# Gated-unit operands loaded by halves: a reordering between retention and the gated unit of a one-core encoder kernel

## The chip, the cores and the metric

The kernel runs on one core of a Trainium2 chip, as one launch. The metric is the device time of a launch in microseconds (us); the median of several runs stands for a kernel. One further execution is taken with the hardware profiler, and all rows of profiles and traces are from that one.

The engines are named as the profile names them: PE is TensorE's matrix multiply (PEld its weight loads), DVE is VectorE, ACT is ScalarE, POOL is GpSimd, and SP is SyncE, whose queue issues all the DMAs of this kernel. L969 is line 969 of the kernel before.

## What is computed

The reference is a trunk of two layers on x of 1024 frames by 1024 channels, in float32. What matters here lies in the first layer. Its input projection gives several streams; one goes through a diagonal state-space layer (S5), a gelu and a gated unit (GLU), another through eight heads of chunkwise retention, and both are joined by an output projection:

```python
def s5_mixer(u, ...):            # ... states, then
    y = jax.nn.gelu(y)
    y = y * jax.nn.sigmoid(y @ glu_w + glu_b)      # the gated unit

def retention(q, k, v):          # per head, DK = 64, DV = 128
    q, k = rope(q) * DK ** -0.5, rope(k)
    scores = einsum('bnihd,bnjhd->bnhij', qc, kc) * intra
    kv = einsum('bnjhd,jh,bnjhe->bnhde', kc, k_dec, vc)
    # s_prev: running sum of kv, decayed from chunk to chunk
    out = scores @ vc + (qc * q_dec) @ s_prev       # then normalised per head

x = x + concatenate([y_s5 * silu(g_s5), y_ret * silu(g_ret)]) @ w_out
```

The second layer (a Conformer convolution module with gates) and a last RMSNorm follow.

## The kernel before

**Layout and products.** Channels lie on the 128 partitions, eight blocks of them (`kb` or `nb`), and frames along the free axis, in two halves of 512 (`h`). Matmuls run on a float32 format with fewer mantissa bits, so each operand is split into a high part (a rounded copy, made on ACT) and a low part (operand minus high part, made on DVE or POOL), and each product is three matmuls: high by high, high by low, low by high (`mm3`, L137 to L144, whose lines L142 to L144 are most of PE's time). `split` (L967 to L969) makes the two parts of an activation: the cast on ACT at L968, the subtraction on DVE at L969. `wload_pieces` (L122) does the same for a weight: a float32 tile `wf` of 128 by 1024 is loaded, cast to `wh` on ACT (L133) and its low part `wl` made on POOL or DVE (L134). `wnext` loads weights two ahead in a fixed list.

**What sets the order.** The kernel is written in a tile language whose scheduler places each engine's instructions in one fixed order, by priority (mostly the order of the program) and by its own estimate of when operands are there. `issue_after(ins)` keeps what is issued under it behind an instruction in that order. Each engine then runs its list strictly in order, and so does SP with its DMAs. A tile has a tag, and a tag has a number of buffers (`bufs`); a new tile waits until the last readers of the tile that had its buffer are done.

**The stretch of the change.** Retention works on pairs of heads (`retention`, L784). `ret_proj` (L809) makes one pair's keys, queries and values. Keys and queries are evacuated to `raw` (L822), four DMAs swap their quarters into `swp` (L831), POOL multiplies both by the rotation tables (L834, L835), and DVE adds them to `krot` and `qrot` (L836). The values are eight blocks of 24 matmuls each (L859 to L861), evacuated on ACT (L862); blocks 0 to 3 read half 0 of the layer's input `xs`, blocks 4 to 7 half 1. `swp` has one buffer. In the same function's wake `y_pass` (L775) loads the output of the S5 part for two channel blocks, takes the gelu on ACT into `yn` (L781, two buffers) and stores it to `yn_d`.

`ret_heads` (L865) then has PE transpose the keys (`ktp`, L874); DVE scales them by the decay (`kt`, L876); PE makes kv (L888), DVE accumulates it to S (L896, L898); PE makes the scores `sp` (L904), DVE masks them to `sc` (L910); PE makes the output from S and from `sc` (L930, L935); DVE normalises (L944 to L950); PE transposes back (L958), and DVE multiplies by the gate (L961).

After the fourth pair comes the gated unit in `layer0_back_and_layer1` (L971). `load_split(yn_d, "y", False)` (L981, L995 to L999) loads the eight rows of gelu output, each 128 by 1024, into buffers of the weights' tag `wf` (three buffers, shared with the weights), and splits each for half 0 and half 1. The operand tiles (`opA`, tags A0 and A1, 16 buffers each) are those that held `xs`: a half's tile comes free when the last V block that reads it has done so. The gated unit's matmuls (`mm_glu`) follow for eight weights and both halves. `yg` and `yn` (L1012 to L1016) are the gate and the gelu output, multiplied on POOL; `sg` (L1020, L1021) is the gate's result.

The scheduler lays the gated unit's first matmuls between the fourth pair's retention products, so that PE has work while DVE makes S and the scores. The loading and scaling of the convolution's weights `convw` (L1101, L1102) stand later in the program, but their load is free to go early, and the scheduler puts the scaling on DVE ahead of the low part `yl0_1`.

Last, `w_out` (L1032) makes x1, stores it, and `h1` (L1048) loads it back for the second layer: for half 0 into tiles of tag `u` (five buffers, eight rows, L1054), normalised by DVE (L1057). Weights used a second time have their low parts stored and loaded back (`wload_again`, L111, L119).

Of the kernel before, what the change touches and what calls it, by code (L numbers as in the profile page):

```python
# [3 lines left out]

# [7 lines left out]
F32 = mybir.dt.float32  # L12
# [27 lines left out]
class Trunk:  # L40
# [734 lines left out]
    def y_pass(self, rp, cb):  # L775

        nc = self.nc
        yt = rp.tile([P, 8, P], F32, name=f"yp_{cb}", tag="yp", bufs=1)
        nc.sync.dma_start(yt[:], self.y_d[cb].rearrange("i h g m -> (h g) i m"))
        yn = rp.tile([P, P, 8], F32, name=f"yn_{cb}", tag="ynt", bufs=2)  # L780
        nc.scalar.activation(yn[:], yt[:].rearrange("p i m -> p m i"), AF.Gelu_apprx_tanh)  # L781
        nc.sync.dma_start(self.yn_d[cb * P:(cb + 1) * P], yn[:].rearrange("p m i -> p (m i)"))

    def retention(self, st):  # L784
        nc, A = self.nc, self.A
        rp = self.rp = self.pool("ret", 1, stack=st)
        early = ExitStack()
        rq = self.rq = self.pool("retq", 1, stack=early, side="right")
        self.rk = rq.tile([P, 2, T], F32, name="ropek")
        nc.sync.dma_start(self.rk[:], A["rope_k"])  # L790
        self.mask = rp.tile([P, NH, P], F32, name="retmask")
        nc.sync.dma_start(self.mask[:], A["ret_mask"])
        self.kdec = rp.tile([P, NH, 64], F32, name="kdec")
        nc.sync.dma_start(self.kdec[:], A["ret_kdec"])
        self.g128 = rp.tile([P, 4], F32, name="g128")
        nc.sync.dma_start(self.g128[:], A["ret_g128"])
        for pair in range(4):
            cur = self.ret_proj(pair)
            with ExitStack() as held:
                if pair:  # L800
                    held.enter_context(self.tc.issue_after(self.last_rs.ins))
                for cb in (2 * pair, 2 * pair + 1):
                    self.y_pass(rq, cb)
            if pair == 3:
                early.close()
                self.lp = self.pool("l1", side="right")
            self.ret_heads(pair, *cur)

    def ret_proj(self, pair):  # L809
        nc, A, rp = self.nc, self.A, self.rp  # L810
        tq = self.rq.tile([P, 2, T], F32, name=f"ropeq_{pair}", tag="ropeq", bufs=1)
        nc.sync.dma_start(tq[:], A["rope_q"][pair])
        raws, tabs = {}, {"k": self.rk, "q": tq}

        def project(nm):
            w = self.wnext(f"{nm}{pair}")
            raw = raws[nm] = self.rq.tile([P, T], F32, name=f"{nm}raw_{pair}", tag="raw", bufs=2)
            for h in range(2):
                c = slice(h * HALF, (h + 1) * HALF)
                ps = self.bank(f"mm_{nm}{pair}_{h}", aux=False)  # L820
                self.gemm(ps[:], w, self.xs[h])
                last = nc.vector.tensor_tensor(raw[:, c], ps[:], self.R[:, c], op=ALU.mult)  # L822
            return last

        def turn(nm, behind=None):
            raw, tab = raws[nm], tabs[nm]
            swp = self.rq.tile([P, T], F32, name=f"{nm}swp_{pair}", tag="swp", bufs=1)
            o = rp.tile([P, T], F32, name=f"{nm}rot_{pair}", tag=f"{nm}rot", bufs=1)
            for b in range(4):
                s = b ^ 1  # L830
                nc.sync.dma_start(swp[32 * b:32 * b + 32, :], raw[32 * s:32 * s + 32, :])  # L831
            cs = [slice(h * HALF, (h + 1) * HALF) for h in range(2)]
            for c in cs:
                nc.gpsimd.tensor_tensor(raw[:, c], raw[:, c], tab[:, 0, c], op=ALU.mult)  # L834
                nc.gpsimd.tensor_tensor(swp[:, c], swp[:, c], tab[:, 1, c], op=ALU.mult)  # L835
            return o, [lambda c=c: nc.vector.tensor_tensor(o[:, c], raw[:, c], swp[:, c], op=ALU.add) for c in cs]  # L836


        project("k")
        krot, adds = turn("k")  # L840
        last = project("q")
        with self.tc.issue_after(last.ins):
            for add in adds:
                add()
        qrot, adds = turn("q")
        for add in adds:
            add()

        wv = [self.wnext(f"v{pair}_{i}") for i in range(2)]
        vt = rp.tile([P, 8, 256], F32, name=f"v_{pair}", tag="v", bufs=2)  # L850
        for b in range(8):
            ps = self.bank(f"mm_v{pair}_{b}", aux=False)
            h, o = b // 4, (b % 4) * P
            for kb in range(KB):
                xh, xl = self.xs[h][kb]
                i, k4 = kb // 4, kb % 4
                wh = wv[i][0][:].rearrange("p (k a) n -> p k (a n)", a=2)[:, k4, :]
                wl = wv[i][1][:].rearrange("p (k a) n -> p k (a n)", a=2)[:, k4, :]
                nc.tensor.matmul(ps[:, :256], xh[:, o:o + P], wh, start=kb == 0, stop=False)  # L859
                nc.tensor.matmul(ps[:, :256], xh[:, o:o + P], wl, start=False, stop=False)  # L860
                nc.tensor.matmul(ps[:, :256], xl[:, o:o + P], wh, start=False, stop=kb == KB - 1)  # L861
            nc.scalar.mul(vt[:, b, :], ps[:, :256], self.Rtok[:, b:b + 1])  # L862
        return krot, qrot, vt

    def ret_heads(self, pair, K, Q, V):  # L865
        nc, rp = self.nc, self.rp
        v = nc.vector

# [1 line left out]
        for hf in range(2):  # L870
            ps = self.bank(f"ktp{hf}_{pair}")
            for b in range(4):
                t0 = (4 * hf + b) * P
                nc.tensor.transpose(ps[:, b * P:(b + 1) * P], K[:, t0:t0 + P], self.ident[:])  # L874
            kd = self.kdec[:, 2 * pair:2 * pair + 2, :].rearrange("p h d -> p (h d)")
            v.tensor_tensor(kt[:, 4 * hf:4 * hf + 4, :], ps[:].rearrange("p (b d) -> p b d", b=4),  # L876
                            kd.unsqueeze(1).broadcast_to([P, 4, P]), op=ALU.mult)

        S = rp.tile([P, 8, P], F32, name=f"S_{pair}", tag="S", bufs=1)
        for hf in range(2):  # L880
# [83 lines left out]
            nc.sync.dma_start(self.yr_d[h * P:(h + 1) * P], gts[hh][:])  # L964


    def split(self, src, hi, lo, eng):  # L967
        self.nc.scalar.copy(hi[:], src)  # L968
        eng.tensor_tensor(lo[:], src, hi[:].bitcast(F32), op=ALU.subtract)  # L969

    def layer0_back_and_layer1(self, st):  # L971
        nc, A = self.nc, self.A
# [8 lines left out]
        def load_split(src, name, halves):  # L981
            res = [[], []]

            def put(kb, h, f):
                a, b = (self.op_tile(self.opA, f"A{h}", f"{name}{q}{kb}_{h}") for q in "hl")
                self.split(f, a, b, v)
                res[h].append((a, b))
            if halves:
                for h in range(2):
                    for kb in range(KB):  # L990
                        f = lp.tile([P, HALF], F32, name=f"{name}f{kb}_{h}", tag="tp", bufs=3)
                        nc.sync.dma_start(f[:], src[rows(kb), hs(h)])
                        put(kb, h, f[:])
            else:
                for kb in range(KB):  # L995
                    f = self.wp.tile([P, T], F32, name=f"{name}f{kb}", tag="wf", bufs=3)
                    nc.sync.dma_start(f[:], src[rows(kb)])
                    for h in range(2):
                        put(kb, h, f[:, hs(h)])  # L999
            return res  # L1000


# [6 lines left out]
        for nb, h in [(nb, h) for nb in range(6) for h in range(2)] + [(6, 0), (7, 0), (6, 1), (7, 1)]:  # L1009
# [11 lines left out]
            v.scalar_tensor_tensor(sg[:], sg[:], 1.0, yg[:], op0=ALU.add, op1=ALU.mult)  # L1021
            a, b = (self.op_tile(opB, f"B{h}", f"ys{q}{nb}_{h}") for q in "hl")
            nc.scalar.mul(a[:], sg[:], 0.5)
            v.scalar_tensor_tensor(b[:], sg[:], 0.5, a[:].bitcast(F32), op0=ALU.mult, op1=ALU.subtract)
            ys[h][nb] = (a, b)
        yr = load_split(self.yr_d, "yr", True)

# [20 lines left out]
        def h1(h):  # L1048
# [2 lines left out]
            res = []  # L1051
            for kb in range(KB):
                t = (opB.tile([P, HALF], F32, name=f"x1n{kb}_{h}", tag="B1") if h else
                     lp.tile([P, HALF], F32, name=f"x1n{kb}_{h}", tag="u", bufs=5))  # L1054
                nc.sync.dma_start(t[:], self.x1_d[rows(kb), hs(h)])
# [43 lines left out]

        cw = lp.tile([P, 8, CONV_K], F32, name="convw")  # L1100
        nc.sync.dma_start(cw[:], A["conv_w"])  # L1101
        v.tensor_scalar(cw[:], cw[:], 0.5, None, op0=ALU.mult)  # L1102
        cv = [[None] * 8 for _ in range(2)]
        zs = [[None] * 8 for _ in range(2)]
        NT = self.TAPS
# [334 lines left out]
```

## Time and profile before

| what | us |
|---|---|
| median of 3 runs | 1219.36 (1218.27 to 1221.7) |
| the profiled execution | 1219.24 |
| its span, first to last instruction | 1217.5 |
| mean granted TensorE clock | 0.997 |

The page gives, for each engine, its busy time and share of the span. The waits list who waited for whom: engine and line, what released it, us in total, how many times and the longest. A row of a timeline has start, length, engine, line, operation, output<-inputs, shapes and a count of merged instructions; in brackets is the engine's idle time before it and what ended that. A row of the chain has start, length, engine and what it was. In the groups by line, `x16 | 12.6, 821 | 3.3 <-ACT yh` means 16 instructions, 12.6 us busy, 821 ns on average, and 3.3 us of idle time before them, ended by ACT's `yh`. A row of a DMA group ends with the median us from issue to landing.

### The profile page before, as it was taken

How to read it: one execution, taken by the hardware profiler on the slowest of the kernel's cores; microseconds unless marked ns; L12 is line 12 of the kernel's file. 1: busy time of each engine (PE TensorE's matmuls, PEld its weight loads, DVE VectorE, ACT ScalarE, POOL GpSimd, SP SyncE). 2: the span in 40 equal slices, each digit the busy share in tenths (PEclk: the TensorE clock that was granted, in tenths of full speed). 3: DMA queues.
4: the chain of work that ended last, by engine and by line, in shares of the span. 5: the costliest groups of instructions: out<-in, count | busy, mean ns of one | idle time of the engine just before them, and what ended most of it. 6: DMA issues, size and time to landing. Idle time of an engine off the chain costs nothing.

```text
span 1217.5 us, 17581 instructions
## 1 busy us (share of the span) xinstructions
PE 1199.5 (99%) x6660; PEld 1011.3 (83%) x6660; DVE 747.1 (61%) x1337; ACT 480.6 (39%) x712; POOL 653.9 (54%) x453
## 2 busy tenths in 40 slices
PE   9999999999999999998999999999999999999997
PEld 7888888888889999997888888788888888888876
DVE  7965555555413635546746101599999799999533
ACT  7212233322222323134434322545545575434652
POOL 2059988888124333342454551578453467758642
PEclk9999999999999999999999999999999999999998
DMA  8342433333384536266446776755677654356764
GB/s 333 104 139 74 152 128 124 133 131 124 107 268 139 176 102 195 82 216 220 165 156 216 269 270 254 260 188 196 222 253 251 232 182 155 123 176 236 243 250 147
DMA packets 98500, 225.03 MB, mean 185 GB/s; under 512 B 9072, under 2 KB 38000, under 8 KB 97776
## 3 DMA queue, kind: packets, MB, share of 16 engines
q1 hardware_dynamic: 98416, 223.92, 54.9%
q8 instruction: 52, 0.85, 0.3%
q14 instruction: 32, 0.26, 0.1%
HBM read 158.41 MB, written 61.28 MB: 180 GB/s over the span
## 4 chain that ended last, share of the span: by engine, by line
PE 91%; DMA 4%; DVE 2%; ACT 1%; POOL 1%; issue 1%; SPq 1%; DVEq 0%; POOLq 0%
PE mm_g L143 7%; PE mm_g L144 7%; PE mm_g L142 7%; PE mm_wo L144 5%; PE mm_wo L142 5%; PE mm_wo L143 5%; PE mm_a L144 2%; PE mm_b L144 2%; PE mm_a L143 2%; PE mm_a L142 2%; PE mm_b L143 2%; PE mm_u L144 2%; PE mm_u L143 2%; PE mm_b L142 2%; PE mm_u L142 2%; PE mm_glu L144 2%
## 5 line engine op out<-in xcount | busy, mean ns | idle before, releaser
L1142 DVE SCALAR_TENSOR_TENSOR cv<-u,convw,cv 128x512 f32<-128x512 f32 x398 | 273.4, 751 | 11.9 <-ACT cv L1128 9.6
L1122 POOL TENSOR_TENSOR tp<-tp,tp 128x512 f32<-128x512 f32 x64 | 83.1, 1298 | 44.4 <-ACT tp L1121 43.3
L144 PE MATMUL mm_g<-xh,wl_g 128*128 128x512 f32 x256 | 100.8, 394 | 0.0
L143 PE MATMUL mm_g<-xl,wh_g 128*128 128x512 f32 x256 | 100.6, 393 | 0.0
L142 PE MATMUL mm_g<-xh,wh_g 128*128 128x512 f32 x256 | 100.5, 393 | 0.0
L861 PE MATMUL mm_v<-wh_v,xl 128*128 128x256 f32 x256 | 72.5, 283 | 0.0
L860 PE MATMUL mm_v<-wl_v,xh 128*128 128x256 f32 x256 | 72.4, 283 | 0.0
L859 PE MATMUL mm_v<-wh_v,xh 128*128 128x256 f32 x256 | 72.4, 283 | 0.0
L134 POOL TENSOR_TENSOR wl_v<-wf_v,wh_v 128x1024 fp32r<-128x1024 f32 x8 | 19.2, 2396 | 88.6 <-ACT wh_v L133 88.6
L1121 ACT ACTIVATE tp<-u,convw 128x512 f32<-128x512 f32 x64 | 45.7, 719 | 34.9 <-POOL tp L1122 33.2
L325 DVE TENSOR_TENSOR gt<-mm_g,R 128x512 f32<-128x512 f32 x32 | 21.9, 685 | 59.9 <-PE mm_g L144 59.9
L143 PEld LDWEIGHTS mm_g<-xl,wh_g 128*128 128x128 f32 x256 | 48.1, 188 | 11.3 <-issue 1.6
L144 PEld LDWEIGHTS mm_g<-xh,wl_g 128*128 128x128 f32 x256 | 48.0, 188 | 10.6
L142 PEld LDWEIGHTS mm_g<-xh,wh_g 128*128 128x128 f32 x256 | 48.1, 188 | 9.6
L144 PE MATMUL mm_oc<-zh,wl_woc 128*128 128x512 f32 (+1 forms) x152 | 54.0, 359 | 1.5 <-DMA wl_woc<-lo_woc 1.5
L1044 DVE TENSOR_TENSOR x<-mm_wo,xr 128x512 f32<-128x512 f32 x16 | 11.1, 692 | 71.9 <-PE mm_wo L144 51.4
L142 PE MATMUL mm_oc<-zh,wh_woc 128*128 128x512 f32 (+1 forms) x152 | 54.3, 363 | 0.0
L143 PE MATMUL mm_oc<-zl,wh_woc 128*128 128x512 f32 (+1 forms) x152 | 53.8, 357 | 0.5 <-POOL zl L969 0.5
L143 PE MATMUL mm_glu<-yl,wh_glu 128*128 128x512 f32 x128 | 50.3, 393 | 2.5 <-DVE yl L969 2.5
L144 PE MATMUL mm_wo<-yrh,wl_wor 128*128 128x512 f32 x128 | 50.0, 391 | 1.4 <-DMA wl_wor<-lo_wor 1.4
L143 PE MATMUL mm_u<-xl,wh_u 128*128 128x512 f32 x128 | 50.1, 391 | 0.8 <-DVE xl L257 0.7
L142 PE MATMUL mm_glu<-yh,wh_glu 128*128 128x512 f32 x128 | 50.1, 393 | 0.6 <-ACT yh L968 0.6
(393 smaller groups left out, 3600.7 us busy)
## 6 DMA issues: line engine op xcount, KB each, us to landing
wf_g<-w_ab SPq DMA_DIRECT2D x16, 512.0 KB, 4.0
wf_wos<-w_out SPq DMA_DIRECT2D x16, 512.0 KB, 5.0
wf_wor<-w_out SPq DMA_DIRECT2D x16, 512.0 KB, 5.8
wf_cb<-w_c SPq DMA_DIRECT2D x16, 512.0 KB, 4.4
wf_ca<-w_c SPq DMA_DIRECT2D x16, 512.0 KB, 4.7
wf_woc<-w_out_c SPq DMA_DIRECT2D x16, 512.0 KB, 5.0
wf_cg<-w_c SPq DMA_DIRECT2D x11, 512.0 KB, 4.4
u_d<-ut SPq DMA_DIRECT2D x8, 512.0 KB, 3.2
```

The costliest lines, as they stand in the source:

```text
L134: lo[i].tensor_tensor(wl[:].rearrange(fl)[:, c], wf[:, c], h.bitcast(F32), op=ALU.subtract)
L142: nc.tensor.matmul(ps, wh[:, kb, :], xh, start=start, stop=False)
L143: nc.tensor.matmul(ps, wh[:, kb, :], xl, start=False, stop=False)
L144: self.last_mm = nc.tensor.matmul(ps, wl[:, kb, :], xh, start=False, stop=stop)
L325: nc.vector.tensor_tensor(gt[:, c], ps[:], self.R[:, c], op=ALU.mult)
L859: nc.tensor.matmul(ps[:, :256], xh[:, o:o + P], wh, start=kb == 0, stop=False)
L860: nc.tensor.matmul(ps[:, :256], xh[:, o:o + P], wl, start=False, stop=False)
L861: nc.tensor.matmul(ps[:, :256], xl[:, o:o + P], wh, start=False, stop=kb == KB - 1)
L1044: v.tensor_tensor(t[:], ps[:], xt[:], op=ALU.add)
L1121: nc.scalar.mul(sk[:], u[:, k:k + HALF], cw[:, nb, k:k + 1])
L1122: gp.tensor_tensor(s0[:], s0[:], sk[:], op=ALU.add)
L1142: v.scalar_tensor_tensor(dst[:], *tap, accs_[i][:], op0=ALU.mult, op1=ALU.add)
```

## The change

Five edits, all but the last around the fourth pair and the gated unit:

1. `load_split` for the gated unit goes half by half: all eight rows of half 0, then those of half 1. Two rows of 128 by 512 share one `wf` buffer, so there are sixteen loads of half the width.
2. `swp` has two buffers, and the gelu's result `yn` one instead of two.
3. For the fourth pair alone the two adds that make `qrot` are held behind the second `kt` (`last_kt`, "behind the decayed keys"); so are the low parts of half 1 (`behind`).
4. The scaling of `convw` is held behind the last low part of the gated unit's result.
5. For half 0 the rows 5 to 7 of x1 are loaded into tag `tp` (three buffers) instead of `u`.

`turned` only keeps a pool open until the held adds are issued. In the order that the scheduler makes of it, PE now does half 0 of the first gated block, but for its last row, ahead of kv, and the rest of it and half 1 in between and behind; before, both halves were mixed as rows came in. On ACT the casts of half 0's rows 0 to 3 stand ahead of the evacuation of V block 3, rows 4 and 5 ahead of that of block 4, rows 6 and 7 ahead of block 5, and `yh0_1` and `wh_glu1` ahead of block 7. On DVE all of half 0's low parts stand ahead of `kt`, then come `qrot`, the low parts 0 to 5 of half 1, S and the scores. On SP the q swaps stand ahead of the second load of a retention gate.

```diff
@@ y_pass
-        yn = rp.tile([P, P, 8], F32, name=f"yn_{cb}", tag="ynt", bufs=2)
+        yn = rp.tile([P, P, 8], F32, name=f"yn_{cb}", tag="ynt", bufs=1)
@@ retention
-            if pair == 3:
-                early.close()
-                self.lp = self.pool("l1", side="right")
-            self.ret_heads(pair, *cur)
+            def turned():
+                if pair == 3:
+                    early.close()
+                    self.lp = self.pool("l1", side="right")
+            self.ret_heads(pair, *cur, turned)
@@ ret_proj
-            swp = self.rq.tile([P, T], F32, name=f"{nm}swp_{pair}", tag="swp", bufs=1)
+            swp = self.rq.tile([P, T], F32, name=f"{nm}swp_{pair}", tag="swp", bufs=2)
...
-        qrot, adds = turn("q")
-        for add in adds:
-            add()
+        qrot, qadds = turn("q")
+        if pair != 3:
+            for add in qadds:
+                add()
+            qadds = ()
@@ ret_heads
-            v.tensor_tensor(kt[:, 4 * hf:4 * hf + 4, :], ps[:].rearrange("p (b d) -> p b d", b=4),
-                            kd.unsqueeze(1).broadcast_to([P, 4, P]), op=ALU.mult)
+            self.last_kt = v.tensor_tensor(kt[:, 4 * hf:4 * hf + 4, :], ps[:].rearrange("p (b d) -> p b d", b=4),
+                                           kd.unsqueeze(1).broadcast_to([P, 4, P]), op=ALU.mult)
+
+        with self.tc.issue_after(self.last_kt.ins):
+            for add in qadds:
+                add()
+        turned()
@@ split
-        eng.tensor_tensor(lo[:], src, hi[:].bitcast(F32), op=ALU.subtract)
+        with self.tc.issue_after(behind.ins) if behind else nullcontext():
+            eng.tensor_tensor(lo[:], src, hi[:].bitcast(F32), op=ALU.subtract)
@@ load_split
-                self.split(f, a, b, v)
+                self.split(f, a, b, v, None if halves or h == 0 else self.last_kt)
...
+            for h in range(2):
                 for kb in range(KB):
-                    f = self.wp.tile([P, T], F32, name=f"{name}f{kb}", tag="wf", bufs=3)
-                    nc.sync.dma_start(f[:], src[rows(kb)])
-                    for h in range(2):
-                        put(kb, h, f[:, hs(h)])
+                    if halves:
+                        f = lp.tile([P, HALF], F32, name=f"{name}f{kb}_{h}", tag="tp", bufs=3)[:]
+                        nc.sync.dma_start(f, src[rows(kb), hs(h)])
+                    else:
+                        if kb % 2 == 0:
+                            f2 = self.wp.tile([P, 2, HALF], F32, name=f"{name}f{kb}_{h}", tag="wf", bufs=3)
+                        f = f2[:, kb % 2, :]
+                        nc.sync.dma_start(f, src[rows(kb), hs(h)])
+                    put(kb, h, f)
@@ gated unit
-            v.scalar_tensor_tensor(b[:], sg[:], 0.5, a[:].bitcast(F32), op0=ALU.mult, op1=ALU.subtract)
+            glu_end = v.scalar_tensor_tensor(b[:], sg[:], 0.5, a[:].bitcast(F32), op0=ALU.mult, op1=ALU.subtract)
@@ h1
-                     lp.tile([P, HALF], F32, name=f"x1n{kb}_{h}", tag="u", bufs=5))
+                     lp.tile([P, HALF], F32, name=f"x1n{kb}_{h}", **({"tag": "u", "bufs": 5} if kb < 5 else
+                                                                     {"tag": "tp", "bufs": 3})))
@@ convw
-        v.tensor_scalar(cw[:], cw[:], 0.5, None, op0=ALU.mult)
+        with self.tc.issue_after(glu_end.ins):
+            v.tensor_scalar(cw[:], cw[:], 0.5, None, op0=ALU.mult)
```

More of the change, by code (lines that the diff above doesn't have):

```diff
@@ L1 @@
 import math
-from contextlib import ExitStack, contextmanager
+from contextlib import ExitStack, nullcontext, contextmanager
 from itertools import chain
@@ L862, in ret_proj, with ret_heads @@
             nc.scalar.mul(vt[:, b, :], ps[:, :256], self.Rtok[:, b:b + 1])
-        return krot, qrot, vt
-    def ret_heads(self, pair, K, Q, V):
+        return krot, qrot, vt, qadds
+    def ret_heads(self, pair, K, Q, V, qadds, turned):
         nc, rp = self.nc, self.rp
@@ L964, in ret_heads, with split @@
             nc.sync.dma_start(self.yr_d[h * P:(h + 1) * P], gts[hh][:])
-    def split(self, src, hi, lo, eng):
+    def split(self, src, hi, lo, eng, behind=None):
         self.nc.scalar.copy(hi[:], src)
-        eng.tensor_tensor(lo[:], src, hi[:].bitcast(F32), op=ALU.subtract)
+        with self.tc.issue_after(behind.ins) if behind else nullcontext():
+            eng.tensor_tensor(lo[:], src, hi[:].bitcast(F32), op=ALU.subtract)
     def layer0_back_and_layer1(self, st):
@@ L985, in put @@
                 a, b = (self.op_tile(self.opA, f"A{h}", f"{name}{q}{kb}_{h}") for q in "hl")
-                self.split(f, a, b, v)
+                self.split(f, a, b, v, None if halves or h == 0 else self.last_kt)
                 res[h].append((a, b))
-            if halves:
-                for h in range(2):
[L990 to L994, printed above, removed]
-                for kb in range(KB):
-                    f = self.wp.tile([P, T], F32, name=f"{name}f{kb}", tag="wf", bufs=3)
-                    nc.sync.dma_start(f[:], src[rows(kb)])
-                    for h in range(2):
-                        put(kb, h, f[:, hs(h)])
+            for h in range(2):
+                for kb in range(KB):
+                    if halves:
[7 more added lines that the diff above has]
+                    put(kb, h, f)
             return res
```

## The prediction, made before the changed kernel was run

> **What bounds the kernel now.** I read the page first (busy times), then the waits of PE, then the timelines of PE, DVE and SP around the longest wait.
>
> ```profile
> PE 1199.5 (99%) x6660; PEld 1011.3 (83%) x6660; DVE 747.1 (61%) x1337; ACT 480.6 (39%) x712; POOL 653.9 (54%) x453
> ```
>
> The kernel is bound by TensorE, and the change alters no matmul. So it can only win the time in which PE waits, or lose by making new waits. The longest entry in the waits of PE lies at the change (us in total, times, longest):
>
> ```profile
> PE mm_glu L143 <- DVE yl L969: 2.5, 3, 1.8
> ```
>
> Idle time understates what is lost, since a matmul's end is modelled: 0.39 us long, while they start 0.23 us apart. So I count from start to start, in the PE timeline:
>
> ```profile
> 554.95 1.04 PE L874 MATMUL ktp<-ident,krot 128*128 128x128 f32 x8
> ...
> 557.00 0.39 PE L144 MATMUL mm_glu<-yh,wl_glu 128*128 128x512 f32 x1
> 557.23 0.40 PE L142 MATMUL mm_glu<-yh,wh_glu 128*128 128x512 f32 x1
> 559.38 0.50 PE L143 MATMUL mm_glu<-yl,wh_glu 128*128 128x512 f32 x1 [1.75 <-DVE yl L969]
> ...
> 561.17 1.09 PE L888 MATMUL kv<-v,kt 128*64 128x128 f32 x16
> ...
> 564.16 0.50 PE L142 MATMUL mm_glu<-yh,wh_glu 128*128 128x512 f32 x1
> ...
> 564.74 0.40 PE L144 MATMUL mm_glu<-yh,wl_glu 128*128 128x512 f32 x1
> 565.75 0.49 PE L142 MATMUL mm_glu<-yh,wh_glu 128*128 128x512 f32 x1 [0.61 <-ACT yh L968]
> 566.48 0.50 PE L143 MATMUL mm_glu<-yl,wh_glu 128*128 128x512 f32 x1 [0.23 <-DVE yl L969]
> ...
> 567.05 0.70 PE L142 MATMUL mm_glu<-yh,wh_glu 128*128 128x512 f32 x2
> 568.26 0.50 PE L143 MATMUL mm_glu<-yl,wh_glu 128*128 128x512 f32 x1 [0.51 <-DVE yl L969]
> ```
>
> 557.23 to 559.38 is 2.15 us for one matmul of 0.23: 1.92 lost. 564.74 to 565.75 loses 0.78, 565.75 to 566.48 loses 0.50, and 567.05 to 568.26 (two matmuls) 0.75. The retention products lose too. The fourth pair's are set beside the third's, which waited for nothing:
>
> ```profile
> 510.13 2.05 PE L935 MATMUL ro<-v,sc 128*128 128x128 f32 x16
> 512.11 1.16 PE L930 MATMUL ro<-S,qrot 64*128 64x128 f32 x16
> 513.20 2.05 PE L935 MATMUL ro<-v,sc 128*128 128x128 f32 x16
> ...
> 570.77 1.04 PE L904 MATMUL sp<-qrot,krot 64*128 64x128 f32 x13
> ...
> 572.52 2.05 PE L935 MATMUL ro<-v,sc 128*128 128x128 f32 x16
> 574.96 1.76 PE L930 MATMUL ro<-S,qrot 64*128 64x128 f32 x16 [0.39 <-DVE S L898]
> 576.65 2.05 PE L935 MATMUL ro<-v,sc 128*128 128x128 f32 x16
> ```
>
> The first L935 group takes 2.44 us instead of 1.98, the L930 group 1.69 instead of 1.09: 1.06 lost. In all 1.92 + 0.78 + 0.50 + 0.75 + 1.06 = **5.0 us** can be won here; as idle it is 2.5 + 0.61 + 0.39 = 3.5.
>
> The busy time of PE's weight loads in that stretch, and in one of equal length before it (length, busy, clock):
>
> ```profile
> 497.46:533.50 36.04, 30.77 (x253) 1.00 0.42 133
> ...
> 554.95:591.03 36.08, 26.00 (x220) 1.00 0.57 192
> ```
>
> [...]
>
> **Why those operands are late.** The chain in order of time names it, and SP's timeline shows the place:
>
> ```profile
> 553.60 4.74 DMA convw<-conv_w
> ...
> 560.37 5.96 DMA yf<-yn_d
> ```
>
> ```profile
> 538.56 2.42 SPq L831 DMA_DIRECT2D qswp<-qraw  x4
> ...
> 559.35 10.06 SPq L997 DMA_DIRECT2D yf<-yn_d  x6
> ```
>
> On DVE the scaling of `convw` (L1102) stood ahead of `yl0_1` and waited for its load until 558.4. Only `yl0_1` and `yl1_1` free the first two `wf` buffers, so loads 2 to 7 of `yf` went out from 559.35 on, one by one, when PE was already at the gated unit. Moreover a full-width row needs both halves' operand slots, and those of half 1 are read by the last V block, until about 555.
>
> **The change part by part.**
>
> *Loads by halves, half 0 first.* V blocks follow each other every 2.88 us (ACT's evacuations, idle and busy):
>
> ```profile
> 549.39 0.47 ACT L862 ACTIVATE v<-mm_v,Rtok 128x256 f32<-128x256 f32 x1 [2.41 <-PE mm_v L861]
> ```
>
> The eighth ends at 554.95, so the fourth, the last to read half 0, starts at 540.6, and half 0's slots come free from then on. In the changed instruction order the loads use two `wf` buffers in turn, since the third holds `glu1` until its low part is made; each load waits for the DVE low part of the load before last. What one costs:
>
> ```profile
> DMA to landing us min/median/max: 3.1/3.5/6.0
> ```
>
> ```profile
> L969 DVE TENSOR_TENSOR yl<-yf,yh 128x512 fp32r<-128x512 f32 x16 | 12.6, 821 | 3.3 <-ACT yh L968 3.3
> L968 ACT CAST yh<-yf 128x512 fp32r<-128x512 f32 x16 | 9.2, 616 | 14.0 <-DMA yf<-yn_d 13.9
> ...
> L134 POOL TENSOR_TENSOR wl_glu<-wf_glu,wh_glu 128x1024 fp32r<-128x1024 f32 x2 | 4.8, 2379 | 21.1 <-ACT wh_glu L133 21.1
> ...
> L910 DVE TENSOR_TENSOR sc<-sp,retmask 128x512 f32<-128x512 f32 x4 | 2.6, 679 | 0.0
> ```
>
> No row shows a half-width `yf`; I take the 3.5 us of a whole one (ends 3.1 and 6.0). Rows 0 to 3 of half 0 are loaded before 542. Their low parts lie beside POOL's query products, where two took long, against 0.68 each alone:
>
> ```profile
> 548.17 3.48 DVE L969 TENSOR_TENSOR yl<-yf,yh 128x512 fp32r<-128x512 f32 x2
> 551.58 0.68 DVE L836 TENSOR_TENSOR qrot<-qraw,qswp 128x512 f32<-128x512 f32 x1
> ...
> 558.64 1.29 DVE L969 TENSOR_TENSOR yl<-yf,yh 128x512 fp32r<-128x512 f32 x2
> ```
>
> At 1.74 each while POOL runs (two or three of them) and 0.65 after, the buffers are free at about 544.6 and 547. The next loads land 3.5 later, and cast and low part of two rows take about 1.9: half 0 is complete at 552.5. PE, which now takes it whole, needs its first row at 555.74 and its seventh at about 560. Three us to spare; the first wait (1.92) and those at 565 to 568 (2.03) go.
>
> *Half 1.* `yf0_1` goes out at about 550 and lands at 553.4. `wh_glu1` stands behind its cast on ACT, and `wl_glu1` (2.38 on POOL) ends at 557.3; only then `yf4_1` can go, landing at 560.8, its two low parts made at 562.4. Queued behind them on DVE are the copies of S and the scores of the fourth pair, and for these PE waits. So this is the place where a new wait can arise. PE comes to it at: 555.74 + 21 matmuls (4.9) = 560.6, kv and first scores 2.99 (561.17 to 564.16), nine matmuls 2.2, the other scores and L930 1.75 (570.77 to 572.52): about 567.7 for the first half's masked scores, and 1.98 + 1.09 later, 570.7, for the second's.
>
> *DVE up to there.* From 555.5: kt 1.3, two qrot 1.2 (behind `wl_glu1`, until 557.3, so 0.6 of waiting), eight `yl` 5.2, seven S (a quarter of the columns; at most half the time) 2.1, four scores 2.7, `sg0_0` 0.7: 13.2 of work and 0.6 of wait, which alone would be 569.3. One more wait is likely: `wl_glu2` runs on POOL from about 566.1 to 568.5, and `yl7_1` or `sg0_0` stands behind it, 1.3 to 2. That gives 570.6 to 571.3 for the second half's scores against 570.7, and 566 for the first half's against 567.7. I take **0.4 us** as what is left of the waits here (ends 0 and 3.0, the latter worked out below).
>
> *Last queries behind the decayed keys, second swap buffer.* The swap of q no longer waits for the keys' rotation; it can leave once the raw queries are evacuated, before 538.56. I take 4 us earlier, POOL's products then end at about 545; with 0 they end as now, before 551. The two adds move behind `kt`, to 558.5; the scores that read them start on PE at 562.4. Nothing is won or lost; without that cover each us beyond 3.9 would cost one. For the other pairs the second buffer lets the swaps go earlier than needed, behind V blocks that keep PE busy.
>
> *One buffer for the gelu's result.* ACT's second gelu of a pair must now wait for the store of the first:
>
> ```profile
> 412.29 2.05 ACT L781 ACTIVATE yn<-yp 128x1024 f32<-128x1024 f32 x1 [4.54 <-DMA yp<-y_d]
> ```
>
> It waits 4.54 us for its own load anyway; the store is issued when the first gelu ends, so one of less than 4.5 us costs nothing, and I take that; a longer one would push the casts behind it on ACT.
>
> *convw after the gated unit.* Its scaling leaves DVE's path; the convolution that reads it comes after all of the gated unit and the output projection: nothing.
>
> *Spare buffers for x1.* Three loads of `x1` no longer wait for the `u` buffers, and leave before the stretch in which PE waits for a weight's low part:
>
> ```profile
> 759.11 3.09 SPq L1055 DMA_DIRECT2D x1n<-x_d  x3
> 763.16 0.32 SPq L119 DMA_DIRECT2D wl_wor<-lo_wor  x1
> ```
>
> ```profile
> 768.11 0.50 PE L144 MATMUL mm_wo<-yrh,wl_wor 128*128 128x512 f32 x1 [1.36 <-DMA wl_wor<-lo_wor]
> ```
>
> ```profile
> wl_wor<-lo_wor SPq DMA_DIRECT2D x8, 512.0 KB, 4.1
> ```
>
> Its issue at 763.16 depends on PE's last use of the buffer, not on the x1 loads, so it stays. But it took 4.9 us to 768.07 with x1 loads in flight; the median of its kind is 4.1. I take the median: **0.8 us** won (ends 0, if it takes 4.9 again, and 1.4, the idle time of the row).
>
> **Sum** against the profiled execution (span 1217.5, 1219.24 with what lies around it; the median of the runs is 1219.36, 0.1 more): 5.0 - 0.4 + 0.8 = 5.4 us, **1213.8 us**. Best case 5.0 + 1.4 and half a us for matmuls after a wait, which start slowly: 1212.3.
>
> **Rivals.** *POOL blocks DVE more than counted.* The 3.48 us for two low parts shows that DVE and POOL hold each other up. POOL has in that stretch the tail of `wl_glu1` (0.6), two `yg` products (half a weight's elements, 1.3 each) and `wl_glu2` (2.4): 5.6 us, of which I count 2.6. If all of it falls on DVE, the scores are 3.0 later, and 5.0 - 3.0 + 0.8 = 2.8 is won: 1216.4. Against it: DVE waits for the load of `yf4_1` about then, which absorbs some. [...]
>
> *The reloads through two buffers are slow, and it gets slower.* Three landings stand in series ahead of DVE's S and scores: `yf4_0`, `yf0_1` and `yf4_1`. The first half's scores have 1.7 us to spare. If each landing takes 6.0 (the longest row) instead of 3.5, the scores are 7.5 - 1.7 = 5.8 late, and the gain of 5.8 is gone: 1219.2. From there on it decides against the change, three us for each us; at 7.5 it is 1223.7. For it: sixteen loads instead of eight, with gate and weight loads between them. Against it: the median is 3.5.
>
> *Nothing is won*: the waits only move to the scores or to the later transposes; about 1219.
>
> **Chances.** Forecast 0.68 (1212.3 to 1215.7), POOL rival 0.17 (to 1217.5, around 1216.4), slow reloads 0.09, nothing won 0.06. A measurement of this kernel can tell about 0.3% (3.7 us) from no change: below 1215.7 faster, above 1223.0 slower. Faster: 0.68 and 0.02 of the POOL rival; slower 0.07 of the reloads and 0.03 for what I don't see; the rest the same. The range 1212.3 to 1217.0 takes the forecast and most of the POOL rival, about 0.8.
>
> **What would show it.** Right: in the waits of PE no `mm_glu <- yl` or `yh`; `yf` loads on SP from 538 to 560 instead of 559 to 569; the fourth pair's output transposes (L958) some 5 us earlier; the wait on `wl_wor` shorter. Wrong: PE's L935 or L930 waiting for `sc` or `S` of DVE by more than 0.5, V blocks of PE waiting for ACT (whose `v` evacuations now stand behind casts of half 0), `yf4_1` landing after 562.5, or a wait later in the gated unit that was not there.

## The result and the profile after

| kernel | median us (runs) | ratio to before, 95% interval |
|---|---|---|
| before | 1219.36 (8) | |
| changed | 1214.18 (8) | 0.9962 [0.9947, 0.9978] |
| changed, second comparison | 1214.44 (12), before 1219.43 (32) | 0.9969 [0.9955, 0.9983] |

The change wins 5.0 to 5.2 us; 5.4 were forecast, against the profiled execution. The profiled execution of the changed kernel took 1218.72, more than its median, so a second profile (1214.58) is read beside it. Lines of the changed kernel are numbered by its own text: V's matmuls L863 to L865, S L905 and L907, `sc` L919, `ro` L939 (by S) and L944 (by `sc`), casts L977, low parts L979.

Waits of PE in the first profile after (us in total, times, longest), without those at both ends of the kernel, which are about as before, and 0.2 for `wl_ca`:

```profile
PE mm_oc L144 <- DMA wl_woc<-lo_woc: 3.3, 2, 1.9
PE mm_wo L144 <- DMA wl_wos<-lo_wos: 1.7, 1, 1.7
...
PE ro L939 <- DVE sc L919: 0.6, 1, 0.6
PE mm_v L863 <- ACT v L866: 0.5, 1, 0.5
```

and in the second:

```profile
PE mm_oc L144 <- DMA wl_woc<-lo_woc: 2.2, 2, 1.8
...
PE ro L939 <- DVE sc L919: 0.9, 1, 0.9
```

The waits of `mm_glu` for `yl` and `yh` (3.1 us before) are gone in both, and so is the wait for `wl_wor`. What is left at this place is `ro` waiting for the scores. SP of the first profile shows the loads where the prediction put them:

```profile
535.18 2.65 SPq L833 DMA_DIRECT2D qswp<-qraw  x4
...
538.85 20.27 SPq L1008 DMA_DIRECT2D yf<-yn_d  x12
...
560.68 0.81 SPq L1008 DMA_DIRECT2D yf<-yn_d  x2
```

**What the stretch won.** Between the first matmul of the fourth pair's V and the first one of `w_out` PE has the same work in every kernel here. Its start and end before:

```profile
531.92 0.28 PE L859 MATMUL mm_v<-wh_v,xh 128*128 128x256 f32 x1
...
660.20 0.39 PE L142 MATMUL mm_wo<-ysh,wh_wos 128*128 128x512 f32 x1
```

and in the second profile after:

```profile
533.17 0.28 PE L863 MATMUL mm_v<-wh_v,xh 128*128 128x256 f32 x1
...
657.95 0.39 PE L142 MATMUL mm_wo<-ysh,wh_wos 128*128 128x512 f32 x1
```

128.28 us became 124.78: 3.50 won (first profile 532.85 to 657.27: 3.86). The experiments below are compared by this stretch, since it leaves out landings ahead of it and behind it that differ between executions: the second profile loses 1.2 ahead of it and wins 2.4 behind it, and the first loses 0.9 ahead and 2.3 behind. Each figure of the stretch is that of one execution, so of two kernels only differences that rows explain are read from it.

**What is left.** PE in the second profile:

```profile
567.27 1.16 PE L913 MATMUL sp<-qrot,krot 64*128 64x128 f32 x14
569.38 1.53 PE L939 MATMUL ro<-S,qrot 64*128 64x128 f32 x12 [0.95 <-DVE sc L919]
570.84 2.05 PE L944 MATMUL ro<-v,sc 128*128 128x128 f32 x16
```

Counted from start to start, the scores and the first output from S take 3.57 us here (567.27 to 570.84), 3.19 in the first profile and 1.75 before (570.77 to 572.52): 1.82 and 1.44 are left, more than the idle 0.95 and 0.58. On DVE:

```profile
567.77 0.69 DVE L979 TENSOR_TENSOR yl<-yf,yh 128x512 fp32r<-128x512 f32 x1 [2.18 <-ACT yh L977]
568.38 0.34 DVE L907 SCALAR_TENSOR_TENSOR S<-S,g,kv 128x128 f32<-128x128 f32 x1
568.64 1.28 DVE L919 TENSOR_TENSOR sc<-sp,retmask 128x512 f32<-128x512 f32 x2
```

DVE isn't overloaded: it sits for 2.18 us behind one low part, `yl6_1`, with the next S and the first scores queued behind it. The load of its row went out at 560.92, as soon as DVE had done `yl0_1` and `yl1_1`, which edit 3 holds behind `kt` and which free a row buffer; the row was cast only at 567.12. The four last `yf` loads took (issue to landing):

```profile
DMA to landing us min/median/max: 3.2/4.8/6.5
```

### The profile page after: what moved, and what is told of

It is laid out like the page before. It is cut to its first block, busy times and chain, and to the rows that moved or that the text cites. A ratio compares the mean times of both kernels' runs of the same rounds, so it can differ in the third digit from the quotient of the medians.

```text
span 1216.9 us, 17600 instructions
## 1 busy us (share of the span) xinstructions
PE 1199.7 (99%) x6660; PEld 1013.1 (83%) x6660; DVE 747.5 (61%) x1337; ACT 478.1 (39%) x710; POOL 653.5 (54%) x453
## 4 chain that ended last, share of the span: by engine, by line
PE 90%; DMA 6%; ACT 1%; DVE 1%; SPq 1%; issue 0%; POOL 0%; DVEq 0%; ACTq 0%
PE mm_g L144 7%; PE mm_g L143 7%; PE mm_g L142 7%; PE mm_wo L144 4%; PE mm_wo L143 4%; PE mm_wo L142 4%; PE mm_a L144 2%; PE mm_b L144 2%; PE mm_b L143 2%; PE mm_a L143 2%; PE mm_a L142 2%; PE mm_u L144 2%; PE mm_b L142 2%; PE mm_u L143 2%; PE mm_v L863 2%; PE mm_v L865 2%
## 5 line engine op out<-in xcount | busy, mean ns | idle before, releaser
L863 PE MATMUL mm_v<-wh_v,xh 128*128 128x256 f32 x256 | 72.5, 283 | 0.5 <-ACT v L866 0.5
L865 PE MATMUL mm_v<-wh_v,xl 128*128 128x256 f32 x256 | 72.4, 283 | 0.0
L144 PE MATMUL mm_wo<-ysh,wl_wos 128*128 128x512 f32 x128 | 49.9, 390 | 1.7 <-DMA wl_wos<-lo_wos 1.7
L1026 POOL TENSOR_TENSOR yg<-yg,yn 128x512 f32<-128x512 f32 x16 | 21.7, 1353 | 54.1 <-DMA yg<-gs_d 21.1
L144 PE MATMUL mm_a<-h1h,wl_ca 128*128 128x512 f32 x128 | 50.3, 393 | 0.2 <-DMA wl_ca<-lo_ca 0.2
```

Source lines behind the costliest of these rows:

```text
L144: self.last_mm = nc.tensor.matmul(ps, wl[:, kb, :], xh, start=False, stop=stop)
L1026: gp.tensor_tensor(yg[:], yg[:], yn[:], op=ALU.mult)
```

## The experiments

The theory at the start (A): the gain is PE's waits at the gated unit, and the halves make it; the swap buffer, the held queries and the gelu buffer only make room. Rivals: the stall on convw makes it (C); the x1 buffers only trade one wait for another (B). Theories D and E came up on the way. Each ratio is to the kernel before as it was run beside that kernel (medians 1219.43, 1219.37 and 1219.03), and lines are numbered by each kernel's own text.

| kernel | median us (runs) | ratio to before | V to `w_out`, won |
|---|---|---|---|
| changed, again | 1214.44 (12) | 0.9969 [0.9955, 0.9983] | 3.50 |
| before + edit 4 (convw) | 1218.19 (12) | 0.9994 [0.9981, 1.0007] | 1.88 |
| before + edit 1 (halves) | 1220.41 (12) | 1.0013 [1.0000, 1.0027] | -1.29 |
| changed without edit 5 (x1) | 1214.76 (9) | 0.9964 [0.9952, 0.9976] | 3.91 |
| changed, one swap buffer | 1219.71 (11) | 1.0004 [0.9992, 1.0016] | -0.19 |
| changed, queries not held | 1218.63 (11) | 0.9995 [0.9985, 1.0004] | 1.16 |
| changed, low parts not held | 1216.46 (10) | 0.9970 [0.9960, 0.9980] | 1.83 |
| changed, `yl6_1`, `yl7_1` behind `sc` | 1214.30 (6) | 0.9963 [0.9951, 0.9975] | 4.24 |
| edits 1 to 3 | 1215.42 (12) | 0.9973 [0.9961, 0.9985] | 4.14 |
| changed, rows at full width | 1218.67 (12) | 0.9996 [0.9982, 1.0010] | 3.01 |
| changed, both scores ahead | 1212.56 (7) | 0.9948 [0.9929, 0.9968] | 5.35 |
| one swap buffer, second profile | 1214.37 (1) | | 2.87 |

**The changed kernel again.** No edit.

> The changed kernel once more, for a second profile. Theory A (the gain is PE's waits at the gated unit; the two new waits of the first profile, 1.7 us for wl_wos and 1.9 more for wl_woc, come from single loads that landed late, 6.9 and 6.4 us): a median of 1213.0 to 1214.5, no wait of mm_glu for yl or yh, and at least one of those two waits gone in this profile. Rival B (the x1 buffers make the wl_wos wait by the order of SP's queue): the wl_wos wait of 1.5 to 2 us is there again, whatever the landing times.

1214.44. The wait for `wl_wos` is gone, that for `wl_woc` 2.2 instead of 3.3. The chain of the first profile had shown how the former came about:

```profile
734.92 9.79 DMA x_d<-x
...
744.78 0.33 SPq L1066
...
746.15 6.92 DMA wl_wos<-lo_wos
```

SP's queue stood at the load of `x1n6_0` (L1066) until the store of x1 ahead of it had landed, 9.79 us after its issue, with `wl_wos` queued behind. PE doesn't wait here in this second profile, so B falls as a fixed wait. But the lateness behind it belongs to edit 5. In all nine profiles with edit 5 the store of x1 took 7.6 to 9.8 us, and `wl_wos` 5.4 to 7.8; in the five without it 5.1 to 5.7, and 3.7 to 3.9. PE waits for `wl_wos` in three of the nine (1.68, and 0.70 and 1.03 below), and in none of the five.

**Edit 4 alone.**

```diff
-        v.tensor_scalar(cw[:], cw[:], 0.5, None, op0=ALU.mult)
+        with self.tc.issue_after(glu_end.ins):
+            v.tensor_scalar(cw[:], cw[:], 0.5, None, op0=ALU.mult)
```

> The kernel before with edit 4 alone: convw's scaling held behind the gated unit. Theory A (convw only starts the lateness; full-width rows still wait for both halves' slots and come one by one through three buffers): the first wait of mm_glu (1.8 us) shrinks, later ones stay; 1.0 to 2.5 us faster than before, 1217 to 1218.4. Rival C (the convw stall alone made the operands late): 4 to 5 us faster, 1214.5 to 1215.5, and no wait for yl over 0.3 us.

1218.19, by its interval not told apart from before; the stretch wins 1.88. The waits for `yl` shrink from 2.5 to 0.8, and PE waits 1.0 for S instead. That is theory A's size; C, which asked for 4 to 5 us, falls.

**Edit 1 alone** (the diff of `load_split`, with `split` as before).

> The kernel before with edit 1 alone: sixteen loads of half width, half 0 first; no holding of low parts, queries or convw, one swap buffer. Theory A (half 0 first is what lets PE go through): 3 to 4.5 us faster than before, 1215 to 1216.4, the waits of mm_glu gone, some of ro's wait for S and sc left. Rival C (convw's scaling is the cause): it now stands in DVE's order behind the second kt, ahead of S, and would hold S and sc; under 1.5 us faster, ro waiting over 2 us.

1220.41: not faster, so **the halves alone don't make the gain**. The waits of `mm_glu` and `ro` are gone, and from `ktp` to `w_out` PE takes 100.36 us instead of 105.25: 4.9 won, the size that A gave to these waits, though PE also comes there 6 us later, which gives the loads time. More than that is lost ahead of `ktp`, where a wait of 3.6 us has come at V:

```profile
PE mm_v L859 <- ACT v L862: 3.6, 1, 3.6
```

Its cause can be followed from SP over DVE to ACT:

```profile
539.37 3.53 SPq L831 DMA_DIRECT2D qswp<-qraw  x4
542.95 9.41 SPq L998 DMA_DIRECT2D yf<-yn_d  x4
```

```profile
547.46 1.77 DVE L836 TENSOR_TENSOR qrot<-qraw,qswp 128x512 f32<-128x512 f32 x1 [8.12 <-POOL qswp L835]
549.15 2.99 DVE L969 TENSOR_TENSOR yl<-yf,yh 128x512 fp32r<-128x512 f32 x3
```

```profile
554.37 0.62 ACT L968 CAST yh<-yf 128x512 fp32r<-128x512 f32 x1 [6.41 <-DMA yf<-yn_d]
...
555.91 0.47 ACT L862 ACTIVATE v<-mm_v,Rtok 128x256 f32<-128x256 f32 x1
```

With one swap buffer the swaps of q leave at 539.37 and POOL's product is late; DVE's add waits for it for 8.12 us, with the low parts that free the row buffers queued behind; so the next rows land late, and V's evacuation stands behind their casts on ACT. Half 0 is loaded early, in the middle of V, so here what delays it delays V. And PE doesn't lose 3.6 us alone: from V's first matmul to `ktp` the stretch is 6.2 us longer (532.51 to 561.72, before 531.92 to 554.95), since the granted clock is 0.50 behind the wait (columns: stretch, length, busy time and count of PE, PEld, DVE, ACT, POOL, clock, DMA share, GB/s):

```profile
556.00:562.00 6.00, 5.57 (x26) 5.57 (x27) 2.41 (x4) 3.19 (x8) 2.72 (x2) 0.50 1.03 377
```

**The changed kernel without edit 5.**

```diff
-                     lp.tile([P, HALF], F32, name=f"x1n{kb}_{h}", **({"tag": "u", "bufs": 5} if kb < 5 else
-                                                                     {"tag": "tp", "bufs": 3})))
+                     lp.tile([P, HALF], F32, name=f"x1n{kb}_{h}", tag="u", bufs=5))
```

> The changed kernel without edit 5: x1's rows 5 to 7 of half 0 in tag u again. Theory A (edit 5 is worth what the prediction gave it, 0.8 us at the wl_wor wait): 0.5 to 1.4 us slower than the changed kernel, a wait of mm_wo for wl_wor of about 1.4. Rival B (edit 5 trades that wait for one on wl_wos): within 0.3 us of the changed kernel. If edit 5 carried the gain: over 3 us slower.

1214.76 against 1214.44: no difference that can be told, and no wait for the load of `wl_wor`. Nor is there one in the kernel of edit 4 alone or that of edits 1 to 3, both with x1 as before; with the halves alone there is one of 1.19. So the 1.36 us that the prediction priced comes in two of the five profiles without edit 5, and the wait for `wl_wos` in three of the nine with it. That is rival B's trade: edit 5 gives one wait that comes at times for another.

**One swap buffer.**

```diff
-            swp = self.rq.tile([P, T], F32, name=f"{nm}swp_{pair}", tag="swp", bufs=2)
+            swp = self.rq.tile([P, T], F32, name=f"{nm}swp_{pair}", tag="swp", bufs=1)
```

> The changed kernel with one swap buffer again; every engine's order is as in the changed kernel, but SP's, where the q swaps stand behind the second gate load and wait for the k swaps' buffer. Theory A (the swap buffer is a condition of the gain: SP's loads of the gelu's rows queue behind the q swaps, some 4 us later, 542.95 instead of 538.85 by the profile of the halves alone; casts stand ahead of V's evacuations, so V waits): mm_v waits 1 to 3.6 us for v, 1215.5 to 1218. The prediction's term (0, off the path): within 0.5 us of the changed kernel.

1219.71: the whole gain is gone, though V waits for nothing. `ro` waits 1.67 us instead of 0.95, which explains 0.7. The rest shows in PE's rows and in the granted clock (columns as above):

```profile
569.27 2.24 PE L939 MATMUL ro<-S,qrot 64*128 64x128 f32 x12 [1.67 <-DVE sc L919]
571.44 3.78 PE L944 MATMUL ro<-v,sc 128*128 128x128 f32 x16
575.15 1.75 PE L939 MATMUL ro<-S,qrot 64*128 64x128 f32 x16
576.82 2.05 PE L944 MATMUL ro<-v,sc 128*128 128x128 f32 x16
```

```profile
570.00:574.00 4.00, 4.00 (x22) 3.78 (x23) 3.65 (x8) 1.93 (x3) 4.00 (x2) 0.50 1.06 408
574.00:578.00 4.00, 4.00 (x32) 3.65 (x32) 3.37 (x21) 0.59 (x2) 0.90 (x2) 0.70 0.88 331
```

Behind the wait the clock was 0.50, and the same 16 matmuls took 3.71 us instead of 1.98. The same kernel, profiled a second time:

> The changed kernel with one swap buffer, a second profile. Theory E (its rows come some 0.8 us later, which lengthens ro's wait for sc to about 1.7 us, and a wait of that length often, not always, halves PE's granted clock for some 6 us, 3 us more): ro waits 1.3 to 2 us again; if the clock stays at 1.00 behind it, the time is 1215 to 1216.5, if it drops to 0.5, 1218 to 1220. Rival F (V waits for its evacuations in most executions, as with the halves alone): a wait of mm_v for v of 1 to 3.6 us.

```profile
568.22 1.53 PE L939 MATMUL ro<-S,qrot 64*128 64x128 f32 x12 [1.60 <-DVE sc L919]
569.68 2.05 PE L944 MATMUL ro<-v,sc 128*128 128x128 f32 x16
571.66 1.19 PE L939 MATMUL ro<-S,qrot 64*128 64x128 f32 x16
572.78 2.05 PE L944 MATMUL ro<-v,sc 128*128 128x128 f32 x16
```

```profile
570.00:574.00 4.00, 4.00 (x43) 3.76 (x41) 4.00 (x15) 1.17 (x2) 3.25 (x2) 1.00 1.05 407
```

The same wait, the clock at 1.00, and 1214.37 us instead of 1218.83. The three groups from the wait on take 4.56 us here and 7.55 there: **2.99 us for the clock**, on top of the wait. This is theory E: the later rows lengthen the wait, and in one of the two executions profiled the clock drops behind it. V waits in neither profile, so rival F, a wait there in most executions, finds no support. Over all timed runs the mean granted clock is 0.9957 with one swap buffer and 0.9974 in the changed kernel; 0.0017 of 1217 us are 2.1 us, an estimate, since that mean also takes in the end of the kernel, where PE is idle and the clock 0.50 (before, from 1212 on). With the 0.7 of wait that makes 2.8 of the 5.3 us between the medians. The other 2.5 stay open: neither profile shows them.

**Queries not held.**

```diff
-        if pair != 3:
-            for add in qadds:
-                add()
-            qadds = ()
+        for add in qadds:
+            add()
+        qadds = ()
```

> The changed kernel, but the two adds of qrot aren't held behind kt in the fourth pair; the low parts still are. Theory A (the first add waits on DVE for POOL's product, 8.1 us in the profile of the halves alone, with the low parts that free the row buffers queued behind it): mm_v waits 2 to 3.6 us for v, 1216 to 1218. The prediction's term (0 for the moved queries): within 0.5 us of the changed kernel.

1218.63, the size of theory A, but at another place: not V, but the scores. DVE waits for the product first and for the rows later:

```profile
544.51 1.77 DVE L838 TENSOR_TENSOR qrot<-qraw,qswp 128x512 f32<-128x512 f32 x1 [4.78 <-POOL qswp L837]
...
563.90 0.69 DVE L978 TENSOR_TENSOR yl<-yf,yh 128x512 fp32r<-128x512 f32 x1 [4.26 <-ACT yh L976]
```

```profile
PE sp L912 <- DVE S L906: 2.3, 1, 2.3
```

**Low parts not held.**

```diff
-                self.split(f, a, b, v, None if halves or h == 0 else self.last_kt)
+                self.split(f, a, b, v)
```

> The changed kernel, but the low parts of half 1 aren't held behind kt; the queries still are. Three of them then stand around the two kt on DVE. Theory A (kt has some 4 us to spare before kv, 557.8 to 561.7, so this half of edit 3 is free): within 0.6 us of the changed kernel. Rival: kt and with it S and sc come later by the low parts and by the casts that they wait for, ro waits 2 us, 1216.

1216.46, the rival's size, but by its interval not told apart from the changed kernel: 0.9970 and 0.9969. What the hold is worth is seen in the profile alone. `yl2_1` stands between the two `kt` and waits for its cast, and S and the scores come late in turn; PE waits 1.23 us, and the clock falls behind it, to 0.56 from 570 to 573:

```profile
556.97 0.68 DVE L880 TENSOR_TENSOR kt<-ktp,kdec 128x512 f32<-128x512 f32 x1
558.86 1.45 DVE L979 TENSOR_TENSOR yl<-yf,yh 128x512 fp32r<-128x512 f32 x1 [1.21 <-ACT yh L977]
560.23 0.68 DVE L880 TENSOR_TENSOR kt<-ktp,kdec 128x512 f32<-128x512 f32 x1
```

```profile
567.74 1.13 PE L913 MATMUL sp<-qrot,krot 64*128 64x128 f32 x14 [1.23 <-DVE S L907]
```

**Last low parts behind the first scores.** `first_sc` is the second `sc` of half 0.

```diff
-                self.split(f, a, b, v, None if halves or h == 0 else self.last_kt)
+                self.split(f, a, b, v, None if halves or h == 0 else self.first_sc if kb >= 6 else self.last_kt)
```

> The changed kernel with the low parts 6 and 7 of half 1 held behind the first two sc instead of behind kt (PE's order is the same). Theory A (the left-over wait of ro, 0.6 and 0.95 us in two profiles, comes from yl6_1 waiting 1.7 and 2.2 us on DVE for its cast, with S and sc queued behind it): ro's wait for sc gone, 0.5 to 0.9 us faster than the changed kernel. Rival (sc itself or S is late by the work ahead): the same time, and ro waits as before.

1214.30, not told apart from the changed kernel. The wait for the first scores is gone, but one of 0.60 has come for the second: `sg0_0`, ahead of them on DVE, waits 1.85 us for ACT. The 0.5 to 0.9 us that were expected are too little for these intervals to tell from nothing.

These runs leave a new theory, D: halves, swap buffer and held queries and low parts are worth something only together.

**Edits 1 to 3 alone.**

> Edits 1 to 3 alone: halves, the second swap buffer (and one gelu buffer), queries and low parts held behind kt; convw and x1 as before. Theory D (these three together are the gain; each alone, or all but one of them, leaves PE another wait): 1213.8 to 1215, within 0.5 us of the changed kernel. Rival (convw's hold and x1's buffers carry part of it): 1216 or more.

1215.42; the stretch wins 4.14, no less than with all five edits, so these three suffice there. The median lies 1 us above the changed kernel's, within the intervals; whether edits 4 and 5 together are worth a part of that isn't settled.

**All but the halves.**

> The changed kernel without edit 1: full-width rows through the three row buffers, all other edits in place. Theory D (both halves' slots are needed for one row, so the rows still come late): 1217 to 1219, PE waiting over 1.5 us for yl, S or sc, with a lower clock after it if the wait is long. Rival (convw and the order on DVE are enough): within 1 us of the changed kernel.

1218.67, the size that D expected, but not by its cause: the stretch still wins 3.01. The profiled execution, 1217.47, is 1.8 faster than that of the kernel before: 1.6 are given back from `w_out` on. Its waits from the stretch on:

```profile
PE mm_glu L143 <- DVE yl L979: 1.4, 1, 1.4
...
PE mm_wo L144 <- DMA wl_wos<-lo_wos: 1.0, 1, 1.0
...
PE mm_wo L142 <- ACT wh_wor L133: 0.9, 1, 0.9
PE mm_wo L144 <- POOL wl_wor L134: 0.8, 1, 0.8
```

Only the one for `wh_wor` is in no other profile. Why these come with the full width stays open, and so does the 1.2 us between this execution and the median. Nor is this the changed kernel but for the width: the scheduler made another order of it, with 9 of the gated matmuls ahead of kv instead of 21. So what the halves are worth by themselves isn't shown.

**Both scores ahead.** The edit of the last low parts, and with it:

```diff
-            v.scalar_tensor_tensor(sg[:], sg[:], 1.0, yg[:], op0=ALU.add, op1=ALU.mult)
+            with self.tc.issue_after(self.last_sc.ins):
+                v.scalar_tensor_tensor(sg[:], sg[:], 1.0, yg[:], op0=ALU.add, op1=ALU.mult)
```

`last_sc` is the last of the four `sc`.

> The changed kernel with the low parts 6 and 7 of half 1 behind the first two sc, and the gated unit's first sg behind the last two (orders of PE, ACT and POOL are the same). Theory A: no wait of ro over 0.3 us, 0.5 to 1 us faster than the changed kernel, 1213.0 to 1213.9. Rival (what is moved back is late for its own readers, or other waits are worth more): within 0.3 us of the changed kernel.

```profile
565.52 0.68 DVE L919 TENSOR_TENSOR sc<-sp,retmask 128x512 f32<-128x512 f32 x1
...
566.98 0.68 DVE L982 TENSOR_TENSOR yl<-yf,yh 128x512 fp32r<-128x512 f32 x1
567.87 0.69 DVE L982 TENSOR_TENSOR yl<-yf,yh 128x512 fp32r<-128x512 f32 x1 [0.21 <-ACT yh L980]
568.48 1.28 DVE L919 TENSOR_TENSOR sc<-sp,retmask 128x512 f32<-128x512 f32 x2
```

1212.56, the fastest of all: 6.5 us below its own before, where the changed kernel lies 5.0 below its own (the intervals overlap). PE waits nowhere in the stretch, which wins 5.35. So what was moved back isn't late for its readers.

## Why the prediction was right, and where it was not

*The 5.0 us that can be won, counted from start to start:* right. The kernel in which PE waits nowhere in the stretch wins 5.35 there; idle time would have said 3.5.

*0.4 us left over:* too small; 1.5 to 1.9 were left (5.35 less 3.86 and 3.50), and the rows of `ro` give 1.44 and 1.82. The place was right: S and scores on DVE behind the low parts of half 1. The step that failed is "only then `yf4_1` can go, landing at 560.8": that load came in time (its cast began at 561.18 and 561.79), but the series had one more member. `yf6_1` went out at 560.68 and 560.92 and took about 6 us, not the 3.5 of the median, in a stretch where the DMA share was 0.93 to 1.03 (second profile, 562 to 570). So the slow-reload rival was half true, for one landing instead of three. The POOL rival wasn't: DVE sat idle ahead of the scores, 1.65 and 2.18 us. Of the waits for POOL in the sum, the one behind `wl_glu1` was there (the two `qrot` took 1.72 us in the first profile, 1.8 were counted); the 1.3 to 2 behind `wl_glu2` wasn't: POOL ran it from 570.93, when `yl7_1` (569.15, 0.68 us) was done.

*Last queries, second swap buffer: nothing won or lost.* Not so: without either one, the gain of the median is gone (1219.71, 1218.63), though of the loss without the swap buffer 2.5 us stay open. Theory D is shown that far: edits 1 to 3 suffice in the stretch, and these two parts are needed; for the held low parts and the halves the times don't settle it. The prediction had the reason in hand, swaps that leave 4 us earlier (3.4 by the profile), but checked it against the scores alone, and not against the loads behind the swaps on SP and the low parts behind the adds on DVE. It also named V waiting for ACT as a sign of failure: that is what came with the halves alone.

*One gelu buffer: nothing.* Not quite. PE waits over 0.4 us at V of the first pair in three of the eleven profiles with one buffer (0.53, 0.94 and 0.42) and in none of the three with two. ACT's second gelu waits 5.6 to 6.2 us for its own load there, instead of 4.4 to 4.7; that the single buffer makes it late isn't shown.

*convw: nothing beyond the stall.* Nothing speaks against it: alone it wins 1.88 in the stretch, and with edits 1 to 3 the stretch has none of it left to win.

*Spare x1 buffers, 0.8:* not won. Without them the median is the same, and the wait for `wl_wor`'s load stays away in three of the four experiments that load x1 as before. The prediction asked what the x1 loads delay where they stood, and not what they delay where they go: `wl_wos`, queued behind them on SP.

**The sum** was right to 0.4 us partly by luck: 3.5 to 3.9 in the stretch instead of 4.6, nothing shown for x1. What else makes 5.0 of the medians, some 1.1 to 1.5, no single profile can say. The granted clock can't either: its mean over the timed runs is 0.9970 before and 0.9974 after, and in profiles without a drop on the way the idle end of the kernel alone moves it between 0.997 and 0.998 (0.50 from 1212 on before; 0.96 and 0.59 from 1206.58 to 1210.91 with one swap buffer, second profile).

## What to carry to other kernels

When loads are moved ahead, list for each engine that they pass what now stands behind them: with the halves alone an early cast stood ahead of V's evacuation, and the move paid only together with a spare buffer and a reordering two engines away. An edit that removes no wait of its own can still decide the gain; price it by what happens without it. And a wait of PE can cost more than its length: behind four of the fifteen of 1.2 us or more the clock dropped, which in the case with both outcomes cost 2.99 us on top of the 1.67.

## What the hardware showed

**The clock after a short wait.** Leaving out both ends of the kernel, PE waited 1.2 us or more 15 times in the 14 profiles. Behind four of them the granted clock fell to about half: 1.23 (low parts not held; 0.56 from 570 to 573), 1.67 (one swap buffer; 0.50 from 570 to 574), 1.93 (first profile after, for `wl_woc`; 0.50 from 1161 to 1163) and 3.61 (halves alone; 0.50 from 556 to 562). Behind the other eleven it stayed at 1.00, among them 2.33 (queries not held), 1.75 (before, and the second profile after) and 1.60 (one swap buffer, second profile). In the case of 1.23 another 0.21 came just before the drop. The case of 1.93, from PE's rows:

```profile
1160.02 0.79 PE L144 MATMUL mm_oc<-zh,wl_woc 128*128 128x512 f32 x1 [1.93 <-DMA wl_woc<-lo_woc]
1160.61 0.63 PE L142 MATMUL mm_oc<-zh,wh_woc 128*128 128x512 f32 x1
1161.04 0.63 PE L143 MATMUL mm_oc<-zl,wh_woc 128*128 128x512 f32 x1
```

Matmuls start every 0.43 us instead of 0.23 until 1163.17. One kernel, that with one swap buffer, got both outcomes (1.67 and 1.60), and the clock dropped behind 1.23 but not behind 1.75. What decides it isn't shown.

**Landings in a busy stretch.** Four loads of 256 KB that went out within 3 us (second profile after, `yf`, 558.6 to 561.3) took 3.2 to 6.5 us, and a store of x1 of 256 KB (first profile) 9.79; a median hides the one that a chain waits for.
